# One core, two-layer hybrid decoder: the embedding's projection moves ahead of the second FFN, and the mixer's output projection runs its upper rows first

## The chip, the cores and the metric

The kernel runs on one core of one Trainium2 chip. The metric is the device time of one launch in microseconds (us). The core has five engines with one instruction stream each: PE (TensorE, the matmuls; its weight loads are shown as PEld), DVE (VectorE), ACT (ScalarE), POOL (GpSimd) and SP (SyncE, which here issues nearly all DMA transfers). Streams run in order; they meet through semaphores.

## The reference, cut to what matters

Per layer (there are two), for 256 tokens of width 1024:

```
x = x + 0.5 * swiglu_ffn(rmsnorm(x, ffn1_norm[i]), ffn1_wi[i], ffn1_wo[i])        # DFF = 2816
z = rmsnorm(x, mix_norm[i]) @ w_in[i]      # split: mq mk mv mo mi mf | sq sk sv | ga gb
hA = mlstm_chunkwise(mq, mk, mv, mi + b_igate, mf + b_fgate)                       # 4 heads
yA = (sigmoid(mo) * rmsnorm(hA, ml_out_norm[i])) @ w_a[i]
yB = swa_sink_attention(sq, sk, sv, ...) @ w_b[i]                                  # window 128, 8 heads
x = x + (sigmoid(ga) * yA + sigmoid(gb) * yB) @ w_out[i]
x = x + 0.5 * swiglu_ffn(rmsnorm(x, ffn2_norm[i]), ffn2_wi[i], ffn2_wo[i])
x = x + sigmoid(rmsnorm(x, ple_norm[i]) @ w_ple_gate[i]) * (p[i] @ w_ple[i])       # p[i]: 256 x 256
```

All of it is float32. The term `p[i] @ w_ple[i]` depends on nothing that the layer computes: it is the "embedding's projection".

## The kernel before, in words

**Products.** Each fp32 operand is split into a high part `hi` (rounded to fp32r by ACT, L227/L291) and a low part `lo` (the rest, by DVE, L229/L292). A product is three matmuls: xh·wl, xl·wh, xh·wh (`mm_unit`, L251 to L253), or in blocks of one kind, hh then hl then lh (`mm_kind`, L261). The 256 tokens are two tiles t = 0, 1; the moving operand is 512 columns of weights.

**Weights.** `specs` is the list of weight units in the order of use; each is 1 MB (4 blocks of 128 rows by 512 columns, or 2 by 1024). A unit lands in one of three `raw` buffers (SP, L213), is split into one of four ring buffers `hi`/`lo`, and is used by 24 matmuls (12 for each t). `take` keeps three units split ahead of use. A `raw` buffer is loaded again once its unit is split; a ring buffer is written again once PE is done with it.

**Turning activations.** A product needs its activations transposed. There are two ways. `turn` (L303 ff.): DVE transposes in 32 x 32 blocks (`inq`, L308), SP writes 256 KB to DRAM (`scr`, L314), SP reads it back rearranged (`back`, L318), then ACT and DVE split it. Or on PE: four 128 x 128 matmuls with the identity (`tp`, L298 and L395) ahead of the split.

**Order.** PE's stream is in the order in which the code is written; a scheduler sets the order of the other engines' streams from it. Side work is written as generators (`spawn`), and every `tick()` after a block of 12 or 24 matmuls advances each of them to its next `yield`. The constants W_... count such ticks. PSUM is eight banks of 512 columns, given out in turn.

**The places that the change touches.** Below, (t,n) is the half n (512 of 1024 columns) of token tile t.
- In `mix_in`: the attention values (`ov`, in `swa_part`) and the mLSTM sums (`num`, in `ml_out`) are fp32 matmuls put between blocks of gate projections, at one place for each t. After the projections `yb`/`ya` (for n = 0, then 1; in each t = 0, 1) the generator `merged` makes ma = sigmoid(ga)·yA + sigmoid(gb)·yB, which is turned into `mT`: n = 0 through DRAM (`mx`), n = 1 on PE (`tp_mx`, L298).
- `out_proj` for `wout`: (t,n) in the order (0,0), (1,0), (0,1), (1,1), each with all 8 row blocks (24 matmuls). After each, `finish` adds into x (L446) and turns that piece for the second FFN, `f2` (`inq_f`, `scr_f`, `back_f`, `xg_f`, `xT_f`), through DRAM; `behind(nxt, ..., near)` says that the last piece goes over PE instead (before: in ffn1 alone).
- `ffn`: its first units are used for both t before the next (`stream_beside`): 48 matmuls on rows 0 to 3, then 48 on rows 4 to 7, t = 0 first in each.
- After `f2`: the embedding's projection `pw` (24 matmuls), copied by ACT (L1128), then the gate product `pg` (`acc_pg`), sigmoid (L1140), product (L1141) and the addition into x (L1142). `pT`, the turned p, is made in the side work of `f2` (`embed`, L1108 ff.).

Of the kernel before, what the change touches and what calls it, by code (L numbers as in the profile page):

```python
# [61 lines left out]
def trunk_kernel(ctx: ExitStack, tc: tile.TileContext, a: dict, out: bass.AP):  # L62
# [527 lines left out]
    def mix_in(pool, i, xn, finish):  # L590
# [240 lines left out]
        Mb = pool.tile([P, MLH, S], F32, name=f"Mb{i}")  # L831
# [266 lines left out]
    for i in range(DEPTH):  # L1098
        nxt = Normed(f"mix{i}", "mix_norm", i)
        ffn(xn, f"f1{i}", behind(nxt, 0.5, near=True), more_constants if i == 0 else None)  # L1100
        xn, nxt = nxt, Normed(f"f2_{i}", "ffn2_norm", i)
        mix(i, xn, behind(nxt, 1.0))
        xn, nxt = nxt, Normed(f"ple{i}", "ple_norm", i)

        with tc.tile_pool(name=f"ple{i}", bufs=1, side="right", reuse_waits="tile") as pool:
            pT = [halves(pool, 2, f"pT{i}_{t}") for t in range(NT)]

            def embed(_):  # L1108
                pin = [pool.tile([P, PDIM], F32, name=f"pin{i}_{t}") for t in range(NT)]
                for t in range(NT):  # L1110
                    nc.sync.dma_start(pin[t], a["p"][i, 0, t * P : (t + 1) * P, :])
                for _ in range(4):
                    yield
# [97 lines left out]
```

## Time and profile before

| | |
|---|---|
| median of 3 runs | 1095.03 us (1094.59 to 1095.68) |
| the profiled execution's own time | 1099.24 us |
| its span in the trace | 1097.5 us |
| granted TensorE clock, mean | 0.999 |
| PE busy | 1088.8 us, 99%, 4942 matmuls |
| DVE, ACT, POOL busy | 774.6 us, 584.9 us, 23.5 us |
| DMA | 260.19 MB, 73.0% of the 16 engines' time |

The page lists busy time by engine, the share of each engine in 40 slices, the chain of work that ended last (followed back from the end, at each step to what released it), and groups of instructions. A timeline row is: start in us, length in us, engine, line, operation, output<-inputs, shapes, count, and in brackets how long the engine had been idle and what ended that. Starts of matmuls are the better measure: a matmul's length is modelled and overlaps the next. In the chain's rows a block's length runs to the next block. SPq rows are the issue of a transfer, not its landing.

### The profile page before, as it was taken

To read this page: it belongs to the slowest core of one execution; us is meant where nothing else is said; L and a number is where in the kernel's file an instruction comes from. 1 tells how busy PE (TensorE), PEld (TensorE's weight loads), DVE (VectorE), ACT (ScalarE), POOL (GpSimd) and SP (SyncE) were. 2 spreads that over 40 slices of the span, in tenths; PEclk is the share of its full clock that TensorE was granted. 3 is DMA by queue.
4 is the path that set the end of the run, shared out by engine and by line. 5 is a ranking of instruction groups with operands and counts; after the bars stand their busy time and mean duration, and the time that the engine had idled before them with its cause. 6 is when DMAs were issued, how large, how long until landed. Compare 5 with 4: busy or idle time off the path is not lost.

```text
span 1097.5 us, 13183 instructions
## 1 busy us (share of the span) xinstructions
PE 1088.8 (99%) x4942; PEld 894.9 (82%) x4942; DVE 774.6 (71%) x969; ACT 584.9 (53%) x842; POOL 23.5 (2%) x28
## 2 busy tenths in 40 slices
PE   9999999999999999999999999999999999999998
PEld 8788888888788888888878888888878788888887
DVE  5776655799697776656876666657986977667554
ACT  4744443778554643444664454437785445544443
POOL 0100000100000000000000000001000000000000
PEclk9999999999999999999999999999999999999999
DMA  8987666686977876866777777667786778777661
GB/s 273 313 281 250 224 211 207 224 285 217 247 235 262 273 236 235 267 202 218 249 240 241 255 222 233 217 199 251 252 244 210 253 262 273 265 240 230 204 224 57
DMA packets 183568, 260.19 MB, mean 237 GB/s; under 512 B 16985, under 2 KB 78545, under 8 KB 183505
## 3 DMA queue, kind: packets, MB, share of 16 engines
q1 hardware_dynamic: 183328, 259.29, 73.0%
q8 instruction: 38, 0.62, 0.2%
q14 instruction: 26, 0.21, 0.1%
q10 hardware_dynamic: 176, 0.07, 0.0%
HBM read 232.05 MB, written 27.28 MB: 236 GB/s over the span
## 4 chain that ended last, share of the span: by engine, by line
PE 91%; DMA 4%; DVE 3%; issue 1%; ACT 1%; DVEq 0%; SPq 0%
PE h_f L251 12%; PE h_f L253 12%; PE h_f L252 12%; PE acc_f_o L253 7%; PE acc_f_o L251 7%; PE acc_f_o L252 7%; PE h_f L261 5%; PE z_mix_sq L261 2%; DMA back_f<-scr_f 2%; PE z_mix_gb L251 1%; PE z_mix_ga L251 1%; PE z_mix_gb L252 1%; PE z_mix_ga L253 1%; PE z_mix_ga L252 1%; PE z_mix_gb L253 1%; PE z_mix_if L261 1%
## 5 line engine op out<-in xcount | busy, mean ns | idle before, releaser
L229 DVE TENSOR_TENSOR lo_f<-raw_f,hi_f 128x1024 fp32r<-128x1024 f32 (+1 forms) x180 | 208.1, 1193 | 59.2 <-ACT hi_f L227 58.9
L227 ACT CAST hi_f<-raw_f 128x1024 fp32r<-128x1024 f32 (+1 forms) x180 | 176.3, 1029 | 108.1 <-PE h_f L253 78.4
L229 DVE TENSOR_TENSOR lo_f_o<-raw_f_o,hi_f_o 128x1024 fp32r<-128x1024 f32 x88 | 104.5, 1218 | 64.8 <-ACT hi_f_o L227 64.8
L227 ACT CAST hi_f_o<-raw_f_o 128x1024 fp32r<-128x1024 f32 x88 | 88.5, 1049 | 97.6 <-PE acc_f_o L253 59.3
L251 PE MATMUL h_f<-lo_f,xT_f_0h 128*128 128x512 f32 x296 | 115.4, 390 | 0.0
L252 PE MATMUL h_f<-hi_f,xT_f_0l 128*128 128x512 f32 x296 | 115.2, 389 | 0.0
L251 PE MATMUL h_f<-lo_f,xT_f_1h 128*128 128x512 f32 x296 | 115.1, 389 | 0.0
L252 PE MATMUL h_f<-hi_f,xT_f_1l 128*128 128x512 f32 x296 | 115.1, 389 | 0.0
L253 PE MATMUL h_f<-hi_f,xT_f_1h 128*128 128x512 f32 x296 | 115.1, 389 | 0.0
L253 PE MATMUL h_f<-hi_f,xT_f_0h 128*128 128x512 f32 x296 | 115.1, 389 | 0.0
L253 PE MATMUL acc_f_o<-hi_f_o,hT_f_1h 128*128 128x512 f32 x176 | 68.5, 389 | 0.0
L251 PE MATMUL acc_f_o<-lo_f_o,hT_f_0h 128*128 128x512 f32 x176 | 68.5, 389 | 0.0
L252 PE MATMUL acc_f_o<-hi_f_o,hT_f_0l 128*128 128x512 f32 x176 | 68.5, 389 | 0.0
L253 PE MATMUL acc_f_o<-hi_f_o,hT_f_0h 128*128 128x512 f32 x176 | 68.5, 389 | 0.0
L251 PE MATMUL acc_f_o<-lo_f_o,hT_f_1h 128*128 128x512 f32 x176 | 68.5, 389 | 0.0
L252 PE MATMUL acc_f_o<-hi_f_o,hT_f_1l 128*128 128x512 f32 x176 | 68.5, 389 | 0.0
L251 PEld LDWEIGHTS h_f<-lo_f,xT_f_0h 128*128 128x128 f32 x296 | 55.6, 188 | 12.2 <-issue 0.6
L253 PEld LDWEIGHTS h_f<-hi_f,xT_f_1h 128*128 128x128 f32 x296 | 55.6, 188 | 11.6
L252 PEld LDWEIGHTS h_f<-hi_f,xT_f_0l 128*128 128x128 f32 x296 | 55.6, 188 | 11.5
L252 PEld LDWEIGHTS h_f<-hi_f,xT_f_1l 128*128 128x128 f32 x296 | 55.5, 188 | 11.6
L251 PEld LDWEIGHTS h_f<-lo_f,xT_f_1h 128*128 128x128 f32 x296 | 55.5, 188 | 11.5
L253 PEld LDWEIGHTS h_f<-hi_f,xT_f_0h 128*128 128x128 f32 x296 | 55.5, 188 | 11.5
(512 smaller groups left out, 2104.0 us busy)
## 6 DMA issues: line engine op xcount, KB each, us to landing
raw_f<-in_ffn_wi_dram SPq DMA_DIRECT2D x78, 1024.0 KB, 5.8
raw_f_o<-in_ffn_wo_dram SPq DMA_DIRECT2D x40, 1024.0 KB, 5.2
raw_f<-in_ffn_wi_dram SPq DMA_DIRECT2D x20, 512.0 KB, 4.6
scr_h_f<-inq_h_f SPq DMA_DIRECT2D x40, 256.0 KB, 3.0
back_h_f<-scr_h_f SPq DMA_DIRECT2D x40, 256.0 KB, 5.2
raw_z_ga<-in_w_in_dram SPq DMA_DIRECT2D x8, 1024.0 KB, 6.0
raw_z_gb<-in_w_in_dram SPq DMA_DIRECT2D x8, 1024.0 KB, 8.1
raw_wout<-in_w_out_dram SPq DMA_DIRECT2D x8, 1024.0 KB, 5.2
```

The lines of the kernel that those rows point to most:

```text
L227: pin(nc.scalar.copy(hi[:, o:e], raw[:, o:e]))
L229: pin(nc.vector.tensor_tensor(lo[:, o:e], raw[:, o:e], hi[:, o:e].bitcast(F32), op=ALU.subtract))
L251: nc.tensor.matmul(o, xh, wl[:, k, sl], start=start, stop=False)
L252: nc.tensor.matmul(o, xl, wh[:, k, sl], start=False, stop=False)
L253: nc.tensor.matmul(o, xh, wh[:, k, sl], start=False, stop=stop)
L261: nc.tensor.matmul(o, xT[k0 + k]["hl".index(c)], w["hl".index(d)][:, k, :], start=k0 + k == 0 and c + d == "hh", stop=done and k0 + k == n ...
```

## The change

- The weight unit `w_ple` comes right after `w_out` and before `ffn2_wi`. The new generator `embedding()` in `mix_in` loads p, turns it in DRAM during the mixer's gate projections, and puts `pT` in the slot of `Mb`. The 24 `pw` matmuls are issued between `wout` and `f2`; ACT copies them from four PSUM banks at the start of `f2`. Behind `f2` the gate product follows at once.
- `wout` is done by rows: rows 0 to 3 for all four (t,n), then rows 4 to 7 for (0,0), (0,1), (1,0), (1,1), with `finish` after each of the latter. The units of `w_out` are listed in that order.
- `merged` turns both halves through DRAM: no `tp_mx` is left.
- `swa_values` for both t is called at one place, and so are the two `ml_out`.
- In layer 0 the last pieces of `f2`, (0,1) and (1,1), go over PE (`near=2`, new `tp_ple`); a tick is added in `out_proj` between the two last units of an FFN's n = 1. W_PLE is 3 instead of 2: the last piece ahead of the next layer is turned on PE one tick later.

```
-W_PLE = 2
+W_PLE = 3
...
-        for n in range(2):
-            specs.extend(by_cols(a["w_out"][i], D, [(512 * n, 512 * (n + 1))], f"wout{i}_{n}"))
+        specs.extend(in_turn([by_cols(a["w_out"][i], D, [(512 * n, 512 * (n + 1))], f"wout{i}_{n}") for n in range(2)]))
+        specs.extend(by_rows(a["w_ple"][i], PDIM, f"wple{i}"))
         specs.extend(ffn_specs(a["ffn2_wi"][i], a["ffn2_wo"][i], f"f2{i}"))
-        specs.extend(by_rows(a["w_ple"][i], PDIM, f"wple{i}"))
...
-                    if unit is not units[0] and n_k == KT:
+                    if unit is not units[0] and (n_k == KT or n == 1):
                         tick()
...
+            values.append((t, turned))
+            if len(values) == NT:
+                for part in values:
+                    swa_values(*part)
...
             for t in range(NT):
                 yield
+            for t in range(NT):
                 spawn(ml_out(t, ha, E01, E2))
...
+        def embedding():
+            pin = work.tile([P, NT, PDIM], F32, tag="sg", name=f"pin{i}")
+            for t in range(NT):
+                nc.sync.dma_start(pin[:, t], a["p"][i, 0, t * P : (t + 1) * P, :])
+            both = pool.tile([P, NT, 2, 2, P], F32R, tag="Mb", name=f"pT{i}")
+            def turned(t):
+                for _ in range(4):
+                    yield
+                inq = work.tile([P, 5 * P], F32, tag="xg", name=f"inq_p{i}_{t}")
+                yield from turn_split(inq, blocks(pin[:, t]), both[:, t, 0], both[:, t, 1], f"p{i}_{t}")
...
         project("ga0", ep_gate(0, AF.Copy))
+        p_parts = embedding()
...
-            if n == 0:
-                yield from back_split(blocks(ma), *part, f"mx{i}_{t}", room)
-                return
-            yield
-            yield
-            with tc.high_priority():
-                transpose_split(ma, 4, part[0], part[1], f"mx{i}_{t}_{n}")
+            yield from back_split(blocks(ma), *part, f"mx{i}_{t}_{n}", room)
...
-        out_proj(f"wout{i}_", KT, [Tiles(p) for p in mT], finish, room)
+        accs = [[bank(f"acc_wout{i}_{t}_{n}") for n in range(2)] for t in range(NT)]
+        for k in range(0, KT, 4):
+            units = [take(f"wout{i}_{n}_{k}") for n in range(2)]
+            for t, n in ((0, 0), (0, 1), (1, 0), (1, 1)):
+                mm_kind(accs[t][n], Tiles(mT[t]), units[n], ["hh", "hl", "lh"], range(4), KT)
+                if k:
+                    finish(t, n, slice(512 * n, 512 * (n + 1)), accs[t][n], room)
+                tick()
+        unit = take(f"wple{i}_0")
+        for t in range(NT):
+            for n in range(2):
+                o = bank(f"pw{i}_{t}_{n}")
+                mm_unit(o, per_tile([p_parts[t]]), unit, 2, slice(512 * n, 512 * (n + 1)))
+                embedded.append(o)
+                tick()
...
-            last = near and t == NT - 1 and n == 1
+            last = n == 1 and t >= NT - near
...
-            ffn(xn, f"f2{i}", behind(nxt, 0.5), embed)
+            ffn(xn, f"f2{i}", behind(nxt, 0.5, near=2 if i < DEPTH - 1 else 0))
```

PE's stream in layer 0, from the first `wout` matmul; first before (names: `acc_wout__t_n`, `mT_t_n` with h or l for high and low part, `hi_wout_n_k`):

```order
L298 MATMUL tp_mx_0_1_2731<-ident,ma_0_1_2695 128x128 x4
L261 MATMUL acc_wout__0_0_2745<-hi_wout_0_0_2570,mT_0_0h 128x512 x4
L261 MATMUL acc_wout__0_0_2745<-lo_wout_0_0_2571,mT_0_0h 128x512 x4
L261 MATMUL acc_wout__0_0_2745<-hi_wout_0_0_2570,mT_0_0l 128x512 x4
L261 MATMUL acc_wout__0_0_2745<-hi_wout_0_4_2652,mT_0_1h 128x512 x4
L261 MATMUL acc_wout__0_0_2745<-lo_wout_0_4_2653,mT_0_1h 128x512 x4
L261 MATMUL acc_wout__0_0_2745<-hi_wout_0_4_2652,mT_0_1l 128x512 x4
L298 MATMUL tp_mx_1_1_2789<-ident,ma_1_1_2738 128x128 x4
```

and now, from the same place:

```order
L260 MATMUL acc_wout_0_0_2766<-hi_wout_0_0_2590,mT_0_0h 128x512 x4
L260 MATMUL acc_wout_0_0_2766<-lo_wout_0_0_2591,mT_0_0h 128x512 x4
L260 MATMUL acc_wout_0_0_2766<-hi_wout_0_0_2590,mT_0_0l 128x512 x4
L260 MATMUL acc_wout_0_1_2767<-hi_wout_1_0_2672,mT_0_0h 128x512 x4
L260 MATMUL acc_wout_0_1_2767<-lo_wout_1_0_2673,mT_0_0h 128x512 x4
L260 MATMUL acc_wout_0_1_2767<-hi_wout_1_0_2672,mT_0_0l 128x512 x4
L260 MATMUL acc_wout_1_0_2768<-hi_wout_0_0_2590,mT_1_0h 128x512 x4
L260 MATMUL acc_wout_1_0_2768<-lo_wout_0_0_2591,mT_1_0h 128x512 x4
L260 MATMUL acc_wout_1_0_2768<-hi_wout_0_0_2590,mT_1_0l 128x512 x4
```

The transposes are gone, and the first use of `mT_0_1` moved from 12 matmuls behind the start to 48 behind it.

DVE's stream in layer 0, where the last merged values are made and `mT_1_0` is split; before:

```order
L979 TENSOR_TENSOR ma_1_1_2738<-ya_1_1_2703,gates_1_1552 128x512
L229 TENSOR_TENSOR lo_wout_1_4_2750<-raw_wout_1_4_2747,hi_wout_1_4_2749 128x1024
L292 TENSOR_TENSOR mT_0_1l<-tp_mx_0_1_2731,mT_0_1h 128x512
L982 TENSOR_TENSOR ma_1_1_2738<-ma_1_1_2738,mbt_1_1_2740 128x512
L229 TENSOR_TENSOR lo_wout_1_4_2750<-raw_wout_1_4_2747,hi_wout_1_4_2749 128x1024
L292 TENSOR_TENSOR mT_1_0l<-back_mx_1_2648,mT_1_0h 128x512
L446 SCALAR_TENSOR_TENSOR x_83<-acc_wout__0_0_2745,x_83 128x512
L308 STREAM_TRANSPOSE inq_f_0_0_0_2797<-x_83 128x512
```

and now (`inq_mx`, `back_mx` by t and n):

```order
L1008 TENSOR_TENSOR ma_1_1_2756<-ma_1_1_2756,mbt_1_1_2758 128x512
L228 TENSOR_TENSOR lo_wout_1_4_2773<-raw_wout_1_4_2770,hi_wout_1_4_2772 128x1024
L307 STREAM_TRANSPOSE inq_mx_1_1_2763<-ma_1_1_2756 128x512
L291 TENSOR_TENSOR mT_1_0l<-back_mx_1_0_2668,mT_1_0h 128x512
L291 TENSOR_TENSOR mT_0_1l<-back_mx_0_1_2723,mT_0_1h 128x512
L228 TENSOR_TENSOR lo_wple_0_2781<-raw_wple_0_2778,hi_wple_0_2780 128x1024 x2
L228 TENSOR_TENSOR lo_f_0_0_0_2845<-raw_f_0_0_0_2842,hi_f_0_0_0_2844 128x1024 x2
L445 SCALAR_TENSOR_TENSOR x_83<-acc_wout_0_0_2766,x_83 128x512
L291 TENSOR_TENSOR mT_1_1l<-back_mx_1_1_2764,mT_1_1h 128x512
L307 STREAM_TRANSPOSE inq_f_0_0_0_2873<-x_83 128x512
```

Two block transposes joined the row ahead of `mT_1_0l`, and the split of `mT_1_1`, which waits for a transfer, stands between x(0,0) and its `inq_f`.

SP's queue in layer 0, from the first `scr_f` of the second FFN (names `f_i_t_n`; `raw_f` are its weights); before:

```order
L314 DMA scr_f_0_0_0_2812<-inq_f_0_0_0_2797 128x512
L213 DMA raw_f_0_1_4_2938<-in_ffn_wi_dram 128x4x512
L318 DMA back_f_0_0_0_2798<-scr_f_0_0_0_2812 128x4x128
L314 DMA scr_f_0_1_0_2861<-inq_f_0_1_0_2827 128x512
L213 DMA raw_f_1_0_0_2946<-in_ffn_wi_dram 128x4x512
L318 DMA back_f_0_1_0_2828<-scr_f_0_1_0_2861 128x4x128
```

and now:

```order
L313 DMA scr_f_0_0_0_2888<-inq_f_0_0_0_2873 128x512
L313 DMA scr_f_0_0_1_2906<-inq_f_0_0_1_2891 128x512
L317 DMA back_f_0_0_0_2874<-scr_f_0_0_0_2888 128x4x128
L313 DMA scr_f_0_1_0_2925<-inq_f_0_1_0_2909 128x512
L212 DMA raw_f_1_0_0_3032<-in_ffn_wi_dram 128x4x512
L317 DMA back_f_0_0_1_2892<-scr_f_0_0_1_2906 128x4x128
L313 DMA scr_f_0_1_1_2947<-inq_f_0_1_1_2928 128x512
L317 DMA back_f_0_1_0_2910<-scr_f_0_1_0_2925 128x4x128
```

The read back of (1,0) now stands behind the write of (1,1). All three streams read the same in layer 1.

More of the change, by code (lines that the diff above doesn't have):

```diff
@@ L583, in attention_constants, with mix, mix_in @@
         nc.vector.tensor_copy(bias, back)
-    def mix(i, xn, finish):
+    def mix(i, xn, finish, embedded):
         with tc.tile_pool(name=f"mix{i}", bufs=1, reuse_waits="tile") as pool:
-            mix_in(pool, i, xn, finish)
-    def mix_in(pool, i, xn, finish):
+            mix_in(pool, i, xn, finish, embedded)
+    def mix_in(pool, i, xn, finish, embedded):
         nm = f"mix{i}"
@@ L771, in swa_logits @@
                 advance(gen)
+        values = []
         def swa_part(t, h0, nh, L, mx, turned):
@@ L813, in swa_part, with swa_values @@
                 yield
+            values.append((t, turned))
+            if len(values) == NT:
+                for part in values:
+                    swa_values(*part)
+        def swa_values(t, turned):
             ov = bank(f"ov{i}_{t}")
@@ L829, in row @@
             return pool.tile([MLH, S], F32, name=f"{name}{i}")
[L831 removed]
+        Mb = pool.tile([P, MLH, S], F32, tag="Mb", name=f"Mb{i}")
         scr = dram.tile([MLH, S], F32, name=f"scr{i}")
@@ L950, in ml_out @@
             yield from back_split(blocks(haf), *ha_tiles(t), f"ha{i}_{t}")
+        def embedding():
[9 more added lines that the diff above has]
+            for t in range(NT):
+                spawn(turned(t))
+            return [(both[:, t, 0], both[:, t, 1]) for t in range(NT)]
         oss = [banks_of(z) for z in ("sq", "if")]
@@ L1000, in mix_in, with behind @@
                 tick()
-        out_proj(f"wout{i}_", KT, [Tiles(p) for p in mT], finish, room)
-    def behind(xn, scale, near=False):
+        accs = [[bank(f"acc_wout{i}_{t}_{n}") for n in range(2)] for t in range(NT)]
[7 more added lines that the diff above has]
+        unit = take(f"wple{i}_0")
+        for t in range(NT):
+            for n in range(2):
[3 more added lines that the diff above has]
+                tick()
+    def behind(xn, scale, near=0):
         def finish(t, n, sl, acc, room):
-            last = near and t == NT - 1 and n == 1
+            last = n == 1 and t >= NT - near
             spawn(xn.piece(t, n, residual(t, sl, acc, scale), *((1,) if last else (0, None, room))))
@@ L1099, in trunk_kernel @@
         nxt = Normed(f"mix{i}", "mix_norm", i)
-        ffn(xn, f"f1{i}", behind(nxt, 0.5, near=True), more_constants if i == 0 else None)
+        ffn(xn, f"f1{i}", behind(nxt, 0.5, near=1), more_constants if i == 0 else None)
         xn, nxt = nxt, Normed(f"f2_{i}", "ffn2_norm", i)
-        mix(i, xn, behind(nxt, 1.0))
+        embedded = []
+        mix(i, xn, behind(nxt, 1.0), embedded)
         xn, nxt = nxt, Normed(f"ple{i}", "ple_norm", i)
         with tc.tile_pool(name=f"ple{i}", bufs=1, side="right", reuse_waits="tile") as pool:
[L1106 to L1113, printed above, removed]
-                for t in range(NT):
-                    inq = work.tile([P, 5 * P], F32, tag="xg", name=f"inq_p{i}_{t}")
-                    yield from turn_split(inq, blocks(pin[t]), *pT[t], f"p{i}_{t}")
-            ffn(xn, f"f2{i}", behind(nxt, 0.5), embed)
-            xn = nxt
             pw = [pool.tile([P, D], F32, name=f"pw{i}_{t}") for t in range(NT)]
-            unit = take(f"wple{i}_0")
             for t in range(NT):
                 for n in range(2):
-                    sl = slice(512 * n, 512 * (n + 1))
-                    o = bank(f"pw{i}_{t}_{n}")
-                    mm_unit(o, per_tile([pT[t]]), unit, 2, sl)
-                    nc.scalar.copy(pw[t][:, sl], o)
-                    tick()
+                    nc.scalar.copy(pw[t][:, 512 * n : 512 * (n + 1)], embedded[2 * t + n])
+            ffn(xn, f"f2{i}", behind(nxt, 0.5, near=2 if i < DEPTH - 1 else 0))
+            xn = nxt
             last = i == DEPTH - 1
```

## The prediction

> **What bounds the kernel now.** I read the page's head first, to see how much there is to win.
>
> ```profile
> span 1097.5 us, 13183 instructions
> PE 1088.8 (99%) x4942; PEld 894.9 (82%) x4942; DVE 774.6 (71%) x969; ACT 584.9 (53%) x842; POOL 23.5 (2%) x28
> PEclk9999999999999999999999999999999999999999
> ```
>
> PE is hardly idle and its clock is full throughout. The change takes no product away, so it can only move what stands between the products: PE's waits, its transposes, and the restarts behind them. PE's waits come next:
>
> ```profile
> PE tp_f L395 <- DVE x L1142: 1.5, 1, 1.5
> PE tp_mx L298 <- DVE ma L982: 0.5, 1, 0.5
> PE acc_wout__0_0_7060 L261 <- DVE mT_1l L292: 0.5, 1, 0.5
> PE h_f L261 <- ACT xT_f_1h L291: 0.5, 1, 0.5
> ```
>
> All four lie at places that the change rewrites, and together they are 3 us. What the transposes cost beyond that is read from the chain of waits around the output projection, layer 0 and then layer 1; the last `ya` matmul of layer 1 is from PE's timeline:
>
> ```profile
> 320.59 0.44 PE tp_mx L298 x4
> 321.03 5.61 PE acc_wout__0_0_2745 L261 x24
> ...
> 332.57 5.44 PE acc_wout__0_1_2830 L261 x24
> ...
> 861.74 0.33 PE tp_mx L298
> ...
> 874.80 5.45 PE acc_wout__0_1_7145 L261 x24
> ```
>
> ```profile
> 860.84 0.39 PE L253 MATMUL ya<-hi_wa,abT 128*128 128x512 f32 x1
> ```
>
> An undisturbed block of 24 matmuls is 5.44 us: 0.227 us each, 2.72 for 12, 0.91 for 4. That is the ruler for what follows.
>
> **The gains.** (a) `tp_mx` goes. In layer 0 two blocks take 332.57 - 320.59 = 11.98 us where 10.88 would do: 1.10 too many, 0.55 for each transpose. In layer 1, from the end of `ya` at 861.23 to 874.80, 13.57 us: 2.69 too many, waits included. Gain 3.8 us, if nothing waits in their place.
>
> (b) The start of `f2`, where PE's timeline shows groups of four that came late (layer 0 twice, then layer 1):
>
> ```profile
> 353.26 1.07 PE L261 MATMUL h_f<-hi_f,xT_f_0l 128*128 128x512 f32 x4
> 354.78 1.19 PE L261 MATMUL h_f<-hi_f,xT_f_1h 128*128 128x512 f32 x4 [0.45 <-ACT xT_f_1h L291]
> ...
> 361.44 1.08 PE L261 MATMUL h_f<-lo_f,xT_f_1h 128*128 128x512 f32 x4
> 362.63 1.21 PE L261 MATMUL h_f<-hi_f,xT_f_1l 128*128 128x512 f32 x4
> ```
>
> ```profile
> 895.49 1.07 PE L261 MATMUL h_f<-hi_f,xT_f_0l 128*128 128x512 f32 x4
> 896.68 1.20 PE L261 MATMUL h_f<-hi_f,xT_f_1h 128*128 128x512 f32 x4
> ```
>
> 0.61 + 0.28 + 0.28 = 1.2 us. These wait for the pieces n = 1, which had three blocks, 16.3 us, between finish and need. Now (0,1) is finished six blocks of 12 into `wout`; two more, the 5.44 us of `pw` and the four blocks of k = 0 lie between it and its need: 21.8 us, and as much for (1,1). Gain 1.2.
>
> (c) The last piece ahead of layer 1, turned on PE (`tp_f`):
>
> ```profile
> 556.37 1.07 PE L261 MATMUL h_f<-hi_f,xT_f_0l 128*128 128x512 f32 x4
> 558.92 0.66 PE L395 MATMUL tp_f<-ident,x 128*128 128x128 f32 x4 [1.48 <-DVE x L1142]
> ```
>
> 2.55 us for a step of 0.91. W_PLE = 3 puts it one block of 12 later, by 2.72 us, which covers the 1.64, and it has two blocks left until it is needed. Gain 1.6.
>
> (d) The attention values of both t stand at one place. From the chain, the first product behind each place:
>
> ```profile
> 277.43 0.43 PE z_mix_gb L251
> 277.85 0.23 PE z_mix_gb L252
> ...
> 282.24 0.43 PE z_mix_gb L251
> ```
>
> One restart of 0.20 fewer in each layer: gain 0.4. Behind `num` I find no such row, so nothing for that.
>
> **The costs.** (e) Two new `tp_ple` in layer 0, at the 0.55 of a `tp_mx`: 1.1. The piece (1,1) must be ready three blocks of 12 behind `f2`'s end; with PE in place of a transfer that is enough. In layer 1 those pieces still go through DRAM, without the 5.44 us of `pw` ahead of them. DVE's timeline there, with the first `pw`:
>
> ```profile
> 1065.45 0.39 PE L251 MATMUL pw<-lo_wple,pT_0h 128*128 128x512 f32 x1
> ```
>
> ```profile
> 1073.96 0.69 DVE L292 TENSOR_TENSOR xT_ple_1l<-xg_ple,xT_ple_1h 128x512 fp32r<-128x512 f32 x1
> ...
> 1076.30 0.69 DVE L292 TENSOR_TENSOR xT_ple_1l<-xg_ple,xT_ple_1h 128x512 fp32r<-128x512 f32 x1
> ```
>
> `pg` would start at 1065.45 and reach rows 4 to 7 two units later, at 1076.3 for t = 0 and 1079.0 for t = 1; the pieces are split at 1074.7 and 1077.0. No cost, with 1.6 us to spare. The `pw` matmuls cost the same in their new place; their ACT copies (four in each layer) stand behind the last `xT_f` split, where PE has 10 us of k = 4 blocks before it needs their banks. p's loads, turns and splits move into the gate projections; they take ACT and SP time there, counted under (f).
>
> (f) A wait in `wout`. `mT` of (1,0) is used from 12 x 2 matmuls in, its low part 1.8 us later: 7.25 us behind the start, at 327.7 in layer 0 and 868.3 in layer 1. Ahead of its split DVE has four times `mbt`, two `ma`, `inq` (two `inq` more than before), eight halves of `w_out`, and `mT` of (0,0):
>
> ```profile
> 306.97 0.68 DVE L981 TENSOR_TENSOR mbt<-yb,gates 128x512 f32<-128x512 f32 x1
> ...
> 310.02 0.66 DVE L981 TENSOR_TENSOR mbt<-yb,gates 128x512 f32<-128x512 f32 x1
> ...
> 849.33 0.69 DVE L981 TENSOR_TENSOR mbt<-yb,gates 128x512 f32<-128x512 f32 x1
> ```
>
> ```profile
> L229 DVE TENSOR_TENSOR lo_wout<-raw_wout,hi_wout 128x1024 fp32r<-128x1024 f32 x8 | 9.6, 1222 | 0.0
> ```
>
> That is 4 x 3.05 + 9.6 + two splits of 0.6 = 23.0 us. Begun at 306.97 it ends at 330.0, 2.3 late; begun at 849.33, at 872.3, 4.0 late. So the upper end is 6.3 us for both layers. The lower is 0: in layer 0 the start hangs on the second turned mLSTM piece,
>
> ```profile
> 300.04 0.62 ACT L291 CAST abT<-back_ha 128x512 fp32r<-128x512 f32 x1 [5.68 <-DMA back_ha<-scr_ha]
> ```
>
> and in the new DVE stream a half of `w_b` (1.2 us by the row of its kind above) stands behind that piece's `inq_ha`, not ahead of it; against that, p's casts now stand ahead of `w_a`'s on ACT. The 23.0 also counts every gap between dependent operations. I take 0.3 and 1.3, together 1.6, nearer the lower end.
>
> (g) A wait for the pieces n = 0 at `f2`. (0,0) is now finished four blocks of 12 plus one into `wout`, 13.6 us ahead of need, and (1,0) likewise. Before, their high parts were split at
>
> ```profile
> 340.53 0.62 ACT L291 CAST xT_f_0h<-xg_f 128x512 fp32r<-128x512 f32 x1 [0.97 <-DVE var_f L425]
> ...
> 346.94 0.62 ACT L291 CAST xT_f_0h<-xg_f 128x512 fp32r<-128x512 f32 x1 [0.83 <-DVE xg_f L411]
> ```
>
> with their sums finished at 326.64 (where the second `tp_mx` began, 5.61 behind 321.03) and 332.57: 14.5 and 15.0 us. So by the nearest rows PE waits 0.9 for the first and 1.4 in all, in each layer 1.4. What decides is the transfers, whose times to landing in that stretch (300 to 366 us) and in the quiet end of the program (1062 to 1076 us) are
>
> ```profile
> scr_f<-inq_f SPq DMA_DIRECT2D x4, 256.0 KB, 3.9
> back_f<-scr_f SPq DMA_DIRECT2D x4, 256.0 KB, 6.2
> scr_mx<-inq_mx SPq DMA_DIRECT2D x2, 256.0 KB, 2.4
> back_mx<-scr_mx SPq DMA_DIRECT2D x2, 256.0 KB, 4.5
> ```
>
> ```profile
> back_ple<-scr_ple SPq DMA_DIRECT2D x2, 256.0 KB, 2.9
> ```
>
> Slow ones share the queue with the 1 MB loads of `raw_f`. In the new order two of these stand ahead of the first `scr_f` and none between it and its read back, so 2.4 + 2.9 is as likely as 3.9 + 6.2, which would make the wait 0. I take 0.6 in each layer, 1.2; ends 0 and 2.8.
>
> The Trainium skill, "DMA: Bandwidth & Descriptors", section "Anatomy of one DMA", fits a transfer on another issue path as about 2.0 us fixed plus its bytes by 436 GB/s: 2.6 us for 256 KB, estimated from that page. That rule speaks against replacing a PE transpose of 0.55 us by two transfers, and it agrees with the quiet rows (2.4 and 2.9), not with the 6.2. By it alone term (g) would be 0 and the sum 1.2 us lower.
>
> **The sum.** -3.8 - 1.2 - 1.6 - 0.4 + 1.1 = -5.9 without new waits; + 1.6 + 1.2 makes -3.1. The profiled execution took 1099.24 us (span 1097.5) and would take 1096.1; it stood 4.2 above the median of the runs, so against the median of 1095.03 the forecast is 1091.9.
>
> **The rivals.** With w for the new waits, the time is 1089.1 + w.
> - No new wait: w = 0, 1089.1. For it: the quiet rows, and room of 21.8 us for the pieces n = 1. Against: DVE's 23 us under (f).
> - The waits eat the gain: (f) at half its upper end, 3.2, and (g) at its 2.8 make w = 6.0, 1095.1. For it: the slow rows. Against: fewer weight loads between the new transfers.
> - Slower: one mechanism, the single SP queue at `f2`. The read back of (1,0) stands behind the write of (1,1), whose `inq_f` stands on DVE behind `xg_f` of (0,0). From (0,0)'s finish: 2.0 to its `inq_f` done, 3.9 and 6.2 for its transfers, 0.7 `xg_f`, 1.1 `inq_f` of (1,1), 0.3 to issue, 6.2 for (1,0) back, 1.3 `xg_f` and split: 21.7 us where need comes after 13.6 + 5.4 = 19.0, so 2.7. If the split of `mT` (1,1), which stands ahead of `inq_f` of (0,0), waits as well (finish to `inq_f` done 4.4 in place of 2.0), it is 5.1 in each layer, and with (f) w = 11.8: 1100.9. It decides from w = 8.1 on, a wait of about 3.3 us in each layer. Against it: both layers must take the slow landings all along.
> - The Trainium skill, "TensorE: Matmul & The Clock Gate", Part 1, says that PE falls to half clock after an idle window of about 3.4 us. No row shows it here, since no wait reached that; it would lengthen only the slower case.
>
> **How the numbers follow.** About 0.2%, 2.2 us, is what a measurement of this kernel tells from no change: faster means w under 3.7, slower w over 8.1. No new wait or nearly (w under 1) 0.15 and the forecast's case (w from 1 to 3.7) 0.40; the gain eaten 0.31; slower 0.14. The forecast's own range is 1090.1 to 1092.8. The range for 8 in 10 starts at 1088.6 (w = 0, and 0.5 of restarts that I did not count) and ends at 1096.5 (w = 7.4, the eaten gain with its end), leaving the slower case out.
>
> **What would show it.** After: no `tp_mx` row; `wout` as eight blocks of 12 at 2.72 us each, with a gap only ahead of `mT` (1,0), by DVE (term f); `f2` straight behind `pw`, with a wait on `xT_f_0h` under 1 us (g), none on `xT_f_1h` (b); no idle time ahead of `tp_f` (c); `pg` of layer 1 without a wait. I am wrong if PE waits over 2 us at `f2` or in `wout`, or if a wait appears at `yb`/`ya`, where I see none.

## The result, and the profile after

The changed kernel takes 1101.05 us (median of 6 runs, 1097.99 to 1108.34), the kernel before 1095.36 (median of 6, 1094.09 to 1097.42): ratio 1.0061, 95% interval 1.0042 to 1.0080. In a second comparison, of 12 runs with 24, it was 1099.87 against 1095.87, ratio 1.0034 (1.0015 to 1.0054). It is 4 to 6 us slower; the forecast was 1091.9, 3.1 faster. The profiled execution is no help by its total: at 1097.99 us it is the shortest of the six, as that of before, 1099.24, was longer than all of its own. So the reading goes by stages. First the page's head, and PE's waits:

```profile
span 1096.2 us, 13195 instructions
PE 1085.9 (99%) x4934; PEld 893.9 (82%) x4934; DVE 778.3 (71%) x971; ACT 584.5 (53%) x842; POOL 26.4 (2%) x28
PEclk9999999999999999999999999999999999999999
```

```profile
PE acc_wout L260 <- ACT mT_0h L290: 2.8, 3, 2.4
PE acc_wout L260 <- DVE mT_0l L291: 2.0, 2, 1.5
...
PE h_f L260 <- DVE lo_f L228: 0.2, 1, 0.2
```

The four waits of before are gone. In their place PE waits 4.8 us in the output projections, for merged values that come back through DRAM. PE's timeline at the start of the output projection shows more than the waits do, layer 0 and then layer 1 (the lines left out are blocks at their usual pace):

```profile
317.20 0.39 PE L252 MATMUL ya<-hi_wa,abT 128*128 128x512 f32 x1
319.98 2.05 PE L260 MATMUL acc_wout<-hi_wout,mT_0h 128*128 128x512 f32 x4 [2.39 <-ACT mT_0h L290]
321.83 1.84 PE L260 MATMUL acc_wout<-lo_wout,mT_0h 128*128 128x512 f32 x4
323.51 1.09 PE L260 MATMUL acc_wout<-hi_wout,mT_0l 128*128 128x512 f32 x4
...
329.60 1.19 PE L260 MATMUL acc_wout<-hi_wout,mT_0l 128*128 128x512 f32 x4 [0.44 <-DVE mT_0l L291]
...
333.37 1.07 PE L260 MATMUL acc_wout<-hi_wout,mT_1h 128*128 128x512 f32 x4
...
859.58 0.39 PE L252 MATMUL ya<-hi_wa,abT 128*128 128x512 f32 x1
860.19 1.19 PE L260 MATMUL acc_wout<-hi_wout,mT_0h 128*128 128x512 f32 x4 [0.22 <-ACT mT_0h L290]
...
869.74 1.21 PE L260 MATMUL acc_wout<-hi_wout,mT_0l 128*128 128x512 f32 x4 [1.52 <-DVE mT_0l L291]
...
873.54 1.07 PE L260 MATMUL acc_wout<-hi_wout,mT_1h 128*128 128x512 f32 x4
```

The upper rows are 48 products, 10.89 us at 0.227. Layer 0 takes 333.37 - 317.43 (the end of `ya`'s slot) = 15.94, so 5.05 are lost: 2.55 until the first product, then 1.7 because the eight products behind the wait take 3.53 us instead of 1.81 (groups of 1.85 and 1.68 us where 0.91 is usual), then 0.8 at the piece (1,0), ahead of its low half. Layer 1 loses 873.54 - 859.81 - 10.89 = 2.84, of which 2.0 at the low half of (1,0) and 0.9 ahead of it. Together 7.9 us. What the forecast expected elsewhere is there: no wait at `tp_f` (560.53 us), none on `xT_f_1h`, and `f2` straight behind `pw`:

```profile
349.85 1.09 PE L260 MATMUL h_f<-hi_f,xT_f_0h 128*128 128x512 f32 x4
...
560.53 0.60 PE L394 MATMUL tp_f<-ident,x 128*128 128x128 f32 x4
```

The chain that comes late is short. (`abT` is the turned input of `yb` and `ya`; its mLSTM half comes through DRAM as `ha`, in one piece for each token tile.) In layer 0: the first `yb` on PE, the split of the second turned mLSTM piece on ACT (what it waited for is its transfer), the first merge on DVE, the split of the first merged piece on ACT.

```profile
295.67 0.39 PE L250 MATMUL yb<-lo_wb,abT_1h 128*128 128x512 f32 x1
299.73 0.62 ACT L290 CAST abT<-back_ha 128x512 fp32r<-128x512 f32 x1 [5.57 <-DMA back_ha<-scr_ha]
307.54 0.69 DVE L1007 TENSOR_TENSOR mbt<-yb,gates 128x512 f32<-128x512 f32 x1
319.31 0.62 ACT L290 CAST mT_0h<-back_mx 128x512 fp32r<-128x512 f32 x1 [9.33 <-DMA back_mx<-scr_mx]
```

PE needs the last of these 21.76 us after the first, at 317.43; it ends at 319.93. The merge's inputs are done at 301.1, but DVE works in order and the merge stands behind the splits of `abT`, `w_b`, p and `w_a`. From the end of the second `abT` split to the end of the first merged piece's split it takes 18.6 to 18.8 us in the three profiles of the kernel before and 19.5 to 19.7 in the two of the changed one, in which p's splits stand between. So the first merged piece follows the second `abT` split nearly one for one.

### The profile page after: what moved, and what is told of

Its sections match the earlier page's. It is cut to its first block, busy times and chain, and to the rows that moved or that the text cites. A ratio compares the mean times of both kernels' runs of the same rounds, so it can differ in the third digit from the quotient of the medians.

```text
span 1096.2 us, 13195 instructions
## 1 busy us (share of the span) xinstructions
PE 1085.9 (99%) x4934; PEld 893.9 (82%) x4934; DVE 778.3 (71%) x971; ACT 584.5 (53%) x842; POOL 26.4 (2%) x28
## 4 chain that ended last, share of the span: by engine, by line
PE 92%; DVE 5%; issue 1%; ACT 1%; DMA 0%; POOL 0%; DVEq 0%; ACTq 0%
PE h_f L250 12%; PE h_f L251 12%; PE h_f L252 12%; PE acc_f_o L250 7%; PE acc_f_o L252 7%; PE acc_f_o L251 7%; PE h_f L260 7%; PE acc_wout L260 3%; PE z_mix_sq L260 1%; PE z_mix_gb L250 1%; PE z_mix_ga L250 1%; PE z_mix_gb L252 1%; PE z_mix_gb L251 1%; PE z_mix_ga L251 1%; PE z_mix_ga L252 1%; DVE lo_wout L228 1%
## 5 line engine op out<-in xcount | busy, mean ns | idle before, releaser
L252 PEld LDWEIGHTS h_f<-hi_f,xT_f_0h 128*128 128x128 f32 x296 | 55.6, 188 | 11.7
```

The lines of the kernel that those rows point to most:

```text
L252: nc.tensor.matmul(o, xh, wh[:, k, sl], start=False, stop=stop)
```

## Experiments

Each run is one profiled execution and its repeats beside runs of the kernel before on the same chip. The table collects what they gave. "Lost" is the time from the first `yb` to the first product of `f2`, over the 43.53 us of the 192 products and, where `pw` stands between, its 5.60 us (layer 0 / layer 1). A wait at the first product of `f2` is thus part of it (0.5 to 1.1 us in a layer of mx_own_queue, lower_rows_by_columns, by_columns_p_not_turned and layer 0 of p_not_turned, nothing elsewhere); later waits of `f2` are not. "abT" is when the split of the high half of the second turned piece ends, "merge" when the first merge starts, both in us after the first `yb`. They are worked out from the timelines of PE, ACT and DVE. Each ratio is to the runs of the kernel before beside it, whose medians are 1095.1 to 1096.6.

| kernel | median us | ratio to before (95%) | lost | abT | merge |
|---|---|---|---|---|---|
| before | 1095.36 | 1 | 1.1 / 2.7 | 2.0 / 3.7 | 8.3 / 10.0 |
| before_again, before_third | one run each: 1092.97, 1095.92 | | 1.1 / 1.3, 1.0 / 0.9 | 2.1 / 2.3, 2.0 / 1.0 | 8.4 / 8.6, 8.3 / 7.3 |
| after | 1101.05 | 1.0061 (1.0042-1.0080) | 5.1 / 2.8 | 4.7 / 2.4 | 11.9 / 9.7 |
| again | 1099.87 | 1.0034 (1.0015-1.0054) | 4.5 / 4.0 | 4.1 / 2.1 | 11.3 / 9.2 |
| mx_own_queue | 1119.6 | 1.0208 (1.0184-1.0231) | 7.9 / 7.3 | 2.3 / 2.2 | 9.8 / 9.4 |
| p_not_turned | 1096.25 | 0.9995 (0.9979-1.0012) | 1.0 / 0.2 | 1.0 / 0.8 | 7.3 / 7.1 |
| sums_apart | 1101.00 | 1.0045 (1.0028-1.0061) | 4.4 / 3.1 | 4.5 / 3.1 | 11.2 / 9.9 |
| lower_rows_by_columns | 1102.77 | 1.0062 (1.0043-1.0081) | 6.8 / 7.6 | 3.2 / 5.9 | 10.5 / 13.1 |
| by_columns_p_not_turned | 1095.61 | 0.9996 (0.9977-1.0016) | 1.6 / 2.6 | 0.8 / 2.0 | 7.1 / 8.3 |
| embedding_alone | 1098.79 | 1.0027 (1.0005-1.0050) | 4.4 / 2.8 | 4.5 / 2.3 | 11.7 / 10.1 |
| slot_and_wple_alone | 1094.80 | 0.9989 (0.9968-1.0009) | 2.2 / 0.9 | 3.2 / 1.7 | 9.5 / 8.0 |
| p_behind | 1101.13 | 1.0042 (1.0022-1.0061) | 5.8 / 2.4 | 4.8 / 2.9 | 11.1 / 9.2 |
| p_transposes_only | 1095.21 | 0.9991 (0.9967-1.0015) | 3.0 / 1.4 | 3.5 / 1.9 | 9.8 / 8.2 |
| p_transfers_only | 1098.58 | 1.0014 (0.9993-1.0036) | 2.3 / 3.4 | 0.2 / 2.9 | 9.1 / 10.3 |
| p_on_pe | 1095.39 | 0.9993 (0.9971-1.0015) | 0.8 / 1.2 | 1.3 / 1.7 | 7.6 / 8.0 |
| before_p_added | 1101.07 | 1.0049 (1.0031-1.0066) | 1.7 / 4.0 | 2.3 / 4.4 | 9.0 / 11.2 |

One profile is one draw: executions of one kernel differ by up to 13 us. The medians carry the verdicts, the profiles the places.

**again.** The changed kernel, unedited.

> The changed kernel once more, for the spread of its times and a second profile. Theory A (the first merged pieces come late through DRAM): PE again waits ahead of the first product of the output projection in layer 0, by 1 to 5 us; where that wait is over 2 us the next eight products take about 0.46 us each instead of 0.227; and the times spread over 3 us or more, because the wait differs from run to run. Theory B (the loss lies elsewhere, at the start of ffn2 or in the opening): that wait is 2.4 us or less as in the first profile, and a new wait of 2 us or more stands at another place.

```profile
PE acc_wout L260 <- DVE mT_0l L291: 3.5, 2, 2.0
PE acc_wout L260 <- ACT mT_0h L290: 2.0, 1, 2.0
```

A profile at the median (1099.90 us), with the same places: 8.5 us lost, of which 2.5 ahead of (1,0) and 6.0 at it; no wait at ffn2's start. The times spread from 1096.70 to 1106.07. Theory A holds, B falls.

**mx_own_queue.**

```diff
-        nc.sync.dma_start(scr, inq[:, 0:n])
+        queue.dma_start(scr, inq[:, 0:n])
...
-        nc.sync.dma_start(dst, bass.AP(...))
+        queue.dma_start(dst, bass.AP(...))
...
-            yield from back_split(blocks(ma), *part, f"mx{i}_{t}_{n}", room)
+            yield from back_split(blocks(ma), *part, f"mx{i}_{t}_{n}", room, nc.gpsimd)
```

> The changed kernel with the eight transfers of the merged values (write and read back) issued on POOL's queue instead of SP's; DVE and ACT keep their order. Theory A1 (the single SP queue delays the read back: 5 us of a load of w_out stand ahead of it): the high half of the first piece is split about 2.5 us earlier, the wait of 2.4 us ahead of the first product in layer 0 goes, and the median falls by 3 to 6 us to 1095-1098. Theory A2 (DVE is late: its low halves stand behind four merges): the wait only moves to the low half (about 2 us, mT l), and the median falls by 1 to 3 us. Theory B: no change within 1 us.

24 us slower than the kernel before. The first read back on POOL's queue, and the split that waited for it:

```profile
313.93 0.77 POOL L317 DMA_DIRECT2D back_mx<-scr_mx  x1 [2.27 <-DMA scr_mx<-inq_mx]
```

```profile
319.33 0.62 ACT L290 CAST mT_0h<-back_mx 128x512 fp32r<-128x512 f32 x1 [8.58 <-DMA back_mx<-scr_mx]
```

Issue to split is 5.4 us, against 5.3 on SP (issued at 314.02, split at 319.31 above). A queue of its own does not shorten that trip. That the transfer waits in the DMA engines, beside the load of `w_out`, and not in SP's queue, is the likely reading; the run does not show where it waits. The Trainium skill, "DMA: Bandwidth & Descriptors", section "Issuing engines are not separate DMA queues", says that all issuers' transfers run on the same 16 DMA engines; this run agrees. POOL's stream is in order too: here the write of (0,1) at 321.25 stands ahead of the read back of (1,0) at 323.51, where SP had issued that read back first. PE's waits are longest at other places, though:

```profile
PE h_f L260 <- ACT xT_f_0h L290: 7.7, 4, 3.1
PE acc_wout L260 <- ACT mT_1h L290: 4.0, 2, 2.0
```

The second is for (1,1), the last merged piece; the first follows at ffn2's start. What part of the 24 us POOL's order has is not shown. A1 and A2 both had the sign wrong.

**p_not_turned.** It leaves out the turn of p; the embedding's product is made of p as it lies.

```diff
-                inq = work.tile([P, 5 * P], F32, tag="xg", name=f"inq_p{i}_{t}")
-                yield from turn_split(inq, blocks(pin[:, t]), both[:, t, 0], both[:, t, 1], f"p{i}_{t}")
+                hi, lo = both[:, t, 0], both[:, t, 1]
+                nc.scalar.copy(hi, blocks(pin[:, t]))
+                nc.vector.tensor_tensor(lo, blocks(pin[:, t]), hi.bitcast(F32), op=ALU.subtract)
```

> The changed kernel without the turn of p: pT is cast and split straight from the loaded p, so that the two transposes on DVE, the two writes and the two reads back are left out (the embedding's product is then made of p as it lies). PE's work is the same. Theory A3 (p's transfers on SP ahead of the second turned mLSTM piece and its splits on DVE and ACT hold up the merges): the second abT split comes about 2.5 us earlier against the first yb product, the merges 3.5 us earlier, the waits in the output projection (5.0 us lost in layer 0, 2.8 in layer 1) fall to under 1.5 us together, and the median falls by 5 to 8 us, to 1093-1096. Rival (the queue order of w_a and DVE's own backlog do it without p): the second abT split stays within 1 us of its place and the median falls by under 2 us.

3.6 us below the changed kernel run beside it (5 to 8 were expected), with 1.2 us lost in place of 8.5, and the whole chain where A3 put it. But it is only level with before: the gains of the forecast do not appear when these waits go. Its profile has others in their place:

```profile
PE h_f L260 <- ACT xT_f_0h L290: 3.5, 2, 3.1
PE lg L758 <- DVE L L765: 1.5, 2, 0.9
```

The first is at ffn2's start, the place of term (g); the second is in the mLSTM's logits, ahead of p's turn in each layer, and stands in seven of the seventeen profiles, one of before among them (before_third, 1.5). Whether these waits hold the gains back in most executions is not shown.

**sums_apart.**

```diff
             for t in range(NT):
                 yield
-            for t in range(NT):
                 spawn(ml_out(t, ha, E01, E2))
```

> The changed kernel with the two mLSTM sums (num and what follows) started one slot apart, as before the change. Theory: the first turned piece comes 2.7 us earlier, but the second, which the merges wait for, stays behind the same load of w_a, so the median changes by less than 1.5 us. Rival (the sums in one slot are what delays the second piece, since ACT and DVE work on both together): the second abT split comes 2 us or more earlier and the median falls by 3 us or more.

As the theory said: the read back of the first piece is issued 10.1 us ahead of `yb` instead of 6.0, the second piece stays, and so does the time.

**lower_rows_by_columns** and **by_columns_p_not_turned.**

```diff
-            for t, n in ((0, 0), (0, 1), (1, 0), (1, 1)):
+            for t, n in ((0, 0), (1, 0), (0, 1), (1, 1)) if k else ((0, 0), (0, 1), (1, 0), (1, 1)):
```

> The changed kernel with the four blocks of the lower rows of w_out in the order (0,0), (1,0), (0,1), (1,1) in place of (0,0), (0,1), (1,0), (1,1): the piece (1,0), needed 5.4 us into ffn2, is finished one block (2.7 us) earlier, and on SP its read back no longer stands behind the write of (1,1). PE's work is the same. Theory C (besides the wait at the start of the output projection there is one of 0 to 8 us, different from run to run, for the piece (1,0) at ffn2's start): the median falls by 2 to 3 us, to 1097-1098, and the slowest times most. Rival (all of the loss is the wait at the start of the output projection): the median stays within 1 us of 1100.

> Both: the lower rows by columns as in lower_rows_by_columns, and p cast and split without its turn as in p_not_turned (its transfers and transposes left out). Theory C with A3 (two places of waiting, each taken away by one of the edits): no wait over 1 us in the output projection or at ffn2's start, and a median of 1091 to 1093, at the lower edge of what p_not_turned gave (1092.0 to 1098.5). Rival (a third place): the median stays at 1095 to 1097.

Theory C's forecasts fail: the first does not get faster (1102.77, above its rival's 1099 to 1101 too), the second stays at 1095.6, as its rival said. Waits of 1 to 3.5 us for `xT_f_0h` at ffn2's start do occur in single profiles of seven variants (3.5 in p_not_turned, 2.3 in p_behind), 7.7 in mx_own_queue, none in the two of the changed kernel. What they cost in the median is open. The profile of the first shows what a long wait costs, in PE's timeline of layer 1:

```profile
862.13 0.39 PE L252 MATMUL ya<-hi_wa,abT 128*128 128x512 f32 x1
866.16 1.88 PE L260 MATMUL acc_wout<-hi_wout,mT_0h 128*128 128x512 f32 x4 [3.64 <-ACT mT_0h L290]
```

**embedding_alone** and **slot_and_wple_alone.**

```diff
-        accs = [[bank(f"acc_wout{i}_{t}_{n}") for n in range(2)] for t in range(NT)]
-        for k in range(0, KT, 4):
-            ...
+        out_proj(f"wout{i}_", KT, [Tiles(p) for p in mT], finish, room)
```

with the transposes of the right half on PE and the order of `w_out`'s loads as before; and, on the kernel before, `W_PLE = 3` with the `values` list of the change.

> The changed kernel with the output projection as before the change (by columns, the merged values of the right half turned on PE); the embedding's turn and product stay between the mixer and ffn2, the attention sums stay in one slot. Theory A3 (p's transfers and splits delay the second turned mLSTM piece and with it the first merged piece): the first product of the output projection waits here as well, 2 us or more in layer 0, and the median is 1098 to 1101. Rival (the new order of the output projection with all pieces through DRAM is what costs): no wait of over 1 us there, and a median of 1093 to 1095.

> The kernel before with W_PLE = 3 and with the attention values of both t in one slot, and nothing else of the change: terms (c) and (d) by themselves, 1.6 + 0.4. Expected: no wait at tp_f ahead of layer 1, one restart fewer in each gb stage, and a median 2.0 us below before's, 1093.5 to 1094.5. Rival: the merged values' pieces, only 1.1 us ahead of their need in layer 0 before, are late once the attention values come late, and nothing is gained (within 0.7 us of before).

The embedding with the old output projection loses 7.2 us at the same place (7.9 and 8.5 in the changed kernel; the 7.2 take in two transposes in each layer, 1.1 us a layer), and is slower than before, by 1.0027 (1.0005 to 1.0050). So the new order of the output projection is not needed for the loss. The two small edits gain nothing that can be measured (0.9989, 0.9968 to 1.0009).

**p_behind**, **before_again**, **before_third.**

```diff
-        nc.sync.dma_start(scr, inq[:, 0:n])
+        held(nc.sync.dma_start(scr, inq[:, 0:n]))
...
+        for t in range(NT):
+            spawn(split_p(t))
         accs = [[bank(f"acc_wout{i}_{t}_{n}") for n in range(2)] for t in range(NT)]
```

where `held` keeps program order and `split_p` does p's splits.

> The changed kernel, whole, with the turn of p started two slots later, its two writes on SP held behind the read back of the second turned mLSTM piece, and its four splits held behind the splits of the merged values (0,0) in the output projection. Theory A3 (p's transfers and splits, where the change put them, delay the second turned piece and the merges): the second abT split ends by 2 us after the first yb product (3.2 to 5.9 us in the changed kernel), the first merge starts by 8.5 us (9.2 to 13.1), PE waits under 1.5 us in both output projections together, and the median is 1095 to 1097, as with p not turned. Rival (leaving the turn out helped because DVE, ACT and the DMA engines had less to do at all, not because of its place): the waits stay at 4 us or more and the median at 1098.5 to 1101.

> The kernel before, for a second profile: the first one took 1099.24 us, 4 us above the median of its runs. If the stretches from which terms (a), (b) and (c) were read (13.57 us from the last ya to the second block of the output projection in layer 1, 1.2 us at ffn2's start, 2.55 us ahead of layer 1's tp_f) are a property of the program, they stand here with the same numbers; if they were delays of that execution, (a) falls to 1.1 in each layer, (b) to about 0, and part of the forecast gain was not there to be had.

> The kernel before, a third profile, with the same question as for before_again: which of the delays that terms (a), (b) and (c) count stand in every execution. Besides: the opening (first 16 products of ffn1 that follow the loads) takes either about 34.0 or about 36.4 us in the profiles so far; expected here one of the two.

Holding p's writes and splits back does not help: the rival of p_behind holds, 1101.13, with PE's waits as without the edit (the 3.2 to 5.9 and 9.2 to 13.1 in the expectation take in lower_rows_by_columns; the changed kernel's own are 2.1 to 4.7 and 9.2 to 11.9):

```profile
PE acc_wout L260 <- DVE mT_0l L291: 3.9, 2, 2.0
PE h_f L260 <- ACT xT_f_0h L290: 2.3, 1, 2.3
PE acc_wout L260 <- ACT mT_0h L290: 1.7, 1, 1.7
```

The edit moves p's writes by little, though. SP's queue in layer 0, where `yb` starts at 295.12 and the split of that second piece at 299.26:

```profile
292.31 0.36 SPq L319 DMA_DIRECT2D back_ha<-scr_ha  x1
292.76 1.34 SPq L315 DMA_DIRECT2D scr_p<-inq_p  x2
```

The writes now stand behind the read back but are under way beside it. So p's place in SP's queue is not what counts; a place outside this stretch was not tried.

The two more profiles of before show how much of the first was that execution. The same chain in before_again, and its wait at `tp_f`:

```profile
296.04 0.39 PE L251 MATMUL yb<-lo_wb,abT_1h 128*128 128x512 f32 x1
297.53 0.62 ACT L291 CAST abT<-back_ha 128x512 fp32r<-128x512 f32 x1 [5.82 <-DMA back_ha<-scr_ha]
304.46 0.68 DVE L981 TENSOR_TENSOR mbt<-yb,gates 128x512 f32<-128x512 f32 x1
316.21 0.62 ACT L291 CAST mT_0h<-back_mx 128x512 fp32r<-128x512 f32 x1 [7.09 <-DMA back_mx<-scr_mx]
317.81 0.60 PE L298 MATMUL tp_mx<-ident,ma 128*128 128x128 f32 x4
...
554.14 0.66 PE L395 MATMUL tp_f<-ident,x 128*128 128x128 f32 x4 [0.78 <-DVE x L1142]
```

The first piece is split at 316.83, 1.0 us before PE is done with `ya` (317.81) and could use it. That margin is all there was; in the six layers of before's three profiles it is 2.1 to -0.7 us. Both values of the opening occur: from 28 us to the first `acc_f_o` before_again takes 102.2 us and before_third 104.7, and every other profile, of both kernels, is near one of the two.

**p_transposes_only**, **p_transfers_only**, **p_on_pe.**

```diff
-                yield from turn_split(inq, blocks(pin[:, t]), both[:, t, 0], both[:, t, 1], f"p{i}_{t}")
+                transpose_split(pin[:, t], 2, both[:, t, 0], both[:, t, 1], f"p{i}_{t}")
```

is p_on_pe; the other two keep only DVE's transpose, or only the trip through DRAM, ahead of the same splits.

> The changed kernel with p's two transposes on DVE and its four splits, but without the trips through DRAM (two writes and two reads left out; the embedding's product is made of the blocks as DVE leaves them). Theory D (the transfers: they take their share of DMA engines that are full here, and the splits wait for them): as p_not_turned, second abT split 1 to 2 us after the first yb, first merge at 7 to 8.5 us, median 1095 to 1097. Theory E (DVE's 1.3 us of transposes ahead of lo_wb and so of the slot that the load of w_a needs): second abT split at 3 us or later, median 1098.5 to 1100.5.

> The changed kernel with p's writes, reads back and splits, but without its two transposes on DVE (p goes to DRAM as it was loaded; the embedding's product is made of that). Theory D: as the changed kernel, first merge at 9.2 us or later, median 1098.5 to 1101. Theory E: first merge at 7 to 8.5 us and a median of 1095 to 1097. If both this and p_transposes_only stay 2 us or more below the changed kernel, the cost is a sum of both shares, with a threshold at the start of the output projection.

> The changed kernel, whole, with p turned on PE (four transposes of 128 by 128 in one slot of the gate projections) instead of through DRAM, and split at once. It takes p off the DMA engines and off DVE's transposes for one restart of PE, 0.5 us in each layer. Expected by both D and E: second abT split by 2 us, first merge by 8.5 us, waits in the output projections under 2 us together, and a median of 1096 to 1098, 2 to 4 us below the changed kernel. Rival (the share that p_not_turned saved was chance): 1099 or more.

Without the trips through DRAM the time is before's (1095.21, and 1095.39 with p turned on PE); with the trips and no transposes it is 1098.58. By the times that points to theory D. But the interval of p_transfers_only, 0.9993 to 1.0036, holds before's time and overlaps those of both others, and both it and p_transposes_only are 2 us or more below the changed kernel by their ratios, which is the sign that the expectation gave for a sum of both shares. In layer 0 the places do not fit D either: in p_transposes_only `abT` comes at 3.5, as E has it, and the merge at 9.8, later than D has it. So how the cost is shared between trips and transposes is open. In p_on_pe PE's waits at the two places are:

```profile
PE h_f L260 <- ACT xT_f_0h L290: 1.1, 1, 1.1
...
PE acc_wout L260 <- DVE mT_0l L291: 0.9, 2, 0.5
```

p_on_pe is the whole computation, 4 to 6 us below the changed kernel, but not clearly below before (0.9971 to 1.0015): no version here is.

**before_p_added.** The kernel before, with the changed kernel's `embedding()` called after `ga0` as well.

> The kernel before with one thing added: the changed kernel's turn of p (loads, transposes, trips through DRAM, splits) at the changed kernel's place in the gate projections, with its result unused; p is still turned and used in ffn2 as before. Theory D (the added traffic at that place is what costs): the second abT split ends 1 to 3 us later after the first yb than before (1.0 to 3.7 there), PE waits 2 us or more for the first merged pieces in one layer at least, and the median rises by 2 to 5 us. Rival (the turn of p costs only together with the new order of the output projection): within 1 us of before.

```profile
PE tp_mx L298 <- DVE ma L1000: 1.7, 1, 1.7
```

```profile
836.50 0.39 PE L251 MATMUL yb<-lo_wb,abT_1h 128*128 128x512 f32 x1
840.30 0.62 ACT L291 CAST abT<-back_ha 128x512 fp32r<-128x512 f32 x1 [5.29 <-DMA back_ha<-scr_ha]
```

4.5 us slower with nothing else of the change, and the second piece is split 4.4 us after `yb` in layer 1 (2.3 in layer 0, within before's 1.0 to 3.7). PE's wait, 1.7 us, is a little under the 2 expected. (It is charged to `ma`; what stands ahead of the transposes' product is the piece `mT_0h`, split 23.7 us after `yb`.) Added to the old order (4.5 us, its loads included) or taken out of the new one (3.6 us), p's turn in this stretch is worth the whole slowdown.

How it costs is seen best at the second read back, `back_ha`. SP's queue in layer 0 of the changed kernel (`yb` starts at 295.67), then of p_not_turned (297.90):

```profile
290.41 0.38 SPq L212 DMA_DIRECT2D raw_wa<-in_w_a_dram  x1
291.28 0.33 SPq L313 DMA_DIRECT2D scr_p<-inq_p  x1
291.71 0.38 SPq L317 DMA_DIRECT2D back_ha<-scr_ha  x1
```

```profile
291.85 0.38 SPq L212 DMA_DIRECT2D raw_wa<-in_w_a_dram  x1
292.70 0.36 SPq L317 DMA_DIRECT2D back_ha<-scr_ha  x1
```

It is issued 4.0 us ahead of `yb` in the first and 5.2 in the second. The means over the layers of each group of profiles:

| profiles | issue ahead of `yb` | issue to split |
|---|---|---|
| before, three | 3.9 (1.9 to 5.2) | 5.5 |
| before_p_added | 2.2 (0.7 and 3.8) | 4.9 |
| the changed kernel, two | 4.0 (3.3 to 4.4) | 6.7 |
| all eight with the whole turn of p here | 3.3 (0.7 to 4.6) | 6.1 |
| the four without p's trips | 4.9 (4.3 to 5.4) | 5.9 |
| p_transfers_only | 4.9 (3.9 and 5.8) | 5.8 |

So p's turn shows in a later issue more than in a slower landing on full DMA engines; in the changed kernel's own two profiles both have a share. Behind it, p's splits add the 0.9 us between 18.7 and 19.6 seen above. The engines are not full in the stretch where p's writes and first read back run, 289 to 302 us: their mean busy share is 0.75 in the changed kernel, 0.64 in p_on_pe, 0.60 in before_again. The loads of `w_a` are no slower with p's turn: in each layer of before, the changed kernel and p_on_pe the first takes 11 to 14 us to land and the second, where its landing is known, 5 to 8.

Why the issue comes late was not tested. In the rows above p's second write stands ahead of the read back; in p_behind it does not, and the read back is issued 2.8 and 3.8 us ahead of `yb` all the same. It stays open.

## Why the prediction was wrong, step by step

The step that failed is (f), "A wait in `wout`". It asked when `mT` of (1,0) would be ready and had DVE begin at 306.97 and 849.33, its old places in time. DVE's own work was sized well: from the first merge to the end of the low half of (1,0) it took 307.54 to 329.55, 22.0 us, where 23.0 was forecast. But DVE's start is not fixed in time: it hangs on the second turned piece, and the change both brings PE to `wout` earlier and puts p's turn into the chain. In before_again the merge starts 8.4 and 8.6 us after `yb`, in the changed kernel 11.9 and 11.3 in layer 0, 9.7 and 9.2 in layer 1. The wait that (f) named, at (1,0) by DVE, did come, and was undersized: 2.7 and 6.0 us (slow products included) against 1.6. The piece (0,0), needed at once, was not asked for at all, though the profile of before had it only 1.0 us early: 318.83 + 0.62 against 320.43; the products ahead of (1,0) lost 5.2 and 2.5 us. The step took 1.6 with an upper end of 6.3; it measured 7.9 and 8.5.

Within it, the sentence that p's turn takes "ACT and SP time there, counted under (f)" put no number on p's turn. Its price is 3.6 us by p_not_turned (two transposes and four transfers in each layer) and 4.5 by before_p_added (two loads and four splits as well).

- (a), 3.8 forecast: the output projection of before loses 2.4 and 1.9 us in the two further profiles. The 2.69 of layer 1 was that execution's wait. The mechanism is right, the size halves.
- (b), 1.2: ffn2's hidden stage takes 119.78 and 120.00 us in before_again, 119.68 twice in before_third, 120.00 and 119.93 after. There was nothing to gain.
- (c), 1.6: the wait at `tp_f` is 0.78 in before_again and none in before_third, by stages 1.2 and 0.1 us more than after. Right that it goes, too large.
- (d), 0.4: the `gb` stage falls from 25.25 to 24.85 in each layer, 0.8, and the stages ahead of it from 80.6 to 80.1 where nothing else waits, where the forecast had "nothing". Larger than forecast. By itself it was worth nothing that can be measured (slot_and_wple_alone); that PE only comes sooner to a chain that did not move is the likely reason, and was not tested.
- (e), 1.1: 0.46 + 0.46 = 0.9 from the stages around layer 0's `tp_ple`, against the two further profiles of before. Right. No wait at `pg` in layer 1, also right.
- (g), 1.2: none in the changed kernel's two profiles, 1 to 3.5 us in several variants with the same `f2`; its size is open. (Of the rows it calls quiet, the 2.4 of `scr_mx` is from the same stretch as the slow ones.) The slower rival had its wait there; it is right about the sign and wrong about the place, so that its 1100.9 is near the measured 1101.05 is luck. "I am wrong if PE waits over 2 us at `f2` or in `wout`" is what happened.

With these sizes the sum is -2.1 - 0.6 - 1.8 + 0.9 = -3.6, and + 8.2 for the waits: 4.6 us slower, within the measured 4.0 to 5.7. With (f) at its 1.6 it would be 2.0 us faster: the sign turned on (f) alone.

The rival by the clock gate was set aside, since no wait would be long enough. In this profile it costs 1.7 us of the 5.05 in layer 0, behind a wait of 2.4.

## What to carry to other kernels

Before work is moved into a stretch, look there for the piece that comes just in time, measure its margin against PE and not in absolute time, and count every instruction and transfer that joins its queues: here the margin was 1.0 us, and before the change PE hardly waited there. Take more than one profile of the kernel before when the gains are a fraction of a per cent: 3.9 of the 7.0 us of gains in (a) to (d) were one execution's delays. A gain ahead of such a chain may be no gain until the chain moves too. And a group's median time to landing can mislead: for `w_a` it is 12.4 us in the changed kernel and 9.9 in p_on_pe but the landing of one of the four loads, a second one, is not known in the first, and the loads that are known are alike.

## What the runs showed of the hardware

The half clock comes after shorter waits than the prediction had it, and not after every one. In the seventeen profiles 26 gaps between PE's matmuls are 2.0 to 4.1 us long from start to start. After eight of them about eight products take 427 ns each instead of 227, some 1.6 us more (in the changed kernel the granted clock is 0.51 from 320.0 to 323.4 us, and full around it): the shortest such gap is 2.19 us (lower_rows_by_columns, layer 0), the longest 4.03. After gaps of 3.44, 3.51 and 3.54 us none is slow. The Trainium skill, "TensorE: Matmul & The Clock Gate", Part 1, has a free-running window of about 3.4 us and half clock after an idle window: eight products at 427 ns are 3.4 us, which agrees with the length, and a window that runs freely fits that gaps alike end differently; that a whole window must be idle does not agree with 2.19 us.
